# A hybrid SSD and gated-conv block on one core: gates beside the scans, sums of y in the merge, first loads by three queues, order at seams

## The chip, the core and the metric

The kernel runs on one core of a Trainium2 chip. The metric is the device time of one execution in microseconds (us). TensorE (PE) multiplies matrices, VectorE (DVE) and ScalarE (ACT) work element by element, GpSimd (POOL) and SyncE (SP) mainly issue transfers here; ACT can issue transfers too. Each engine runs its own instructions strictly in the order in which they were written. Where one needs another's result it waits on a semaphore, and everything behind it on its engine waits with it.

## What is computed

One block over 1024 tokens of width 1024, all in float32 (from the reference, cut):

```
u = rmsnorm(h) @ w_in
z, xbc, dt, s_b, s_c, s_x, g_a, g_b = split(u)
xbc = silu(conv(xbc)); y = scan(xbc, dt) + d_skip * xs
y = y * silu(z)
yg = y.reshape(4 groups); y = yg * rsqrt(mean(yg * yg) + eps) * w
branch_a = y @ w_ssd_proj
branch_b = (s_b * conv(s_c * s_x)) @ w_sconv_proj
h = h + (sigmoid(g_a) * branch_a + sigmoid(g_b) * branch_b) @ w_o
h = h + (silu(n @ w_gate) * (n @ w_up)) @ w_down       # n = rmsnorm(h)
return rmsnorm(h)
```

## The kernel before

**Matmuls.** A float32 product is three fp32r matmuls: each operand is split into an upper part (ACT, a copy) and a lower part (DVE, a subtraction; `split`, L73/L74 and L76/L77), and upper x upper, upper x lower and lower x upper are added (`mm3`, L81 to L83; `mmc`, L679 to L681). A matmul is 128x128 by 128x512.

**Pairs.** Most of the first projection is computed in `Pair`s: two slabs of 128 columns by Strassen's scheme with seven products in place of eight. A product is 4 blocks of 128 x 3 matmuls, so a pair takes 7 x 12 = 84 matmuls where two direct slabs take 96. The operands made of rows (B11, T1, T2 and so on) are split once by `put` and read by all pairs. The three first pairs (z 0 to 5) run with their products interleaved while the second half of the rows is still being turned and split (`second_half`, called from the loop over the first 21 products); the others follow one by one.

**Direct slabs and the scan.** 20 slabs are computed directly (`direct_tile`): z 12 to 15 and the 16 slabs of the two gates. Beside them runs the scan: 4 groups x 8 chunks of 128 tokens are 32 items of two parts each (`part1`, `part2`), a generator from which `direct_tile` takes a step after a matmul triple whenever `due` has grown: `due = turn * 65 // (len(direct) * 16 - 4)`. After each half of a group (4 chunks) a `norm` generator starts: it loads z, multiplies, squares, sums over the group by PE (`pq`), makes 1/sqrt (`rstd_of`), turns it by PE (`prt`), writes it to memory and reads it back spread over all partitions (`rbc`), scales y with it (L543) and writes y (`y_g`). With the second half of a group it makes four sums of y for the Strassen scheme of the merge (L557) and writes them (`yt_d`, L558).

**The merge.** `ms` is a stream of chunks of 24 matmuls: 14 of `gv` (conv branch), 28 of `gy` (scan branch), then `go` (w_o). `ms.step()` loads four chunks ahead, splits two ahead (two operands, so two ACT copies and two DVE subtractions for each chunk) and does one chunk of matmuls. Between chunks `pump_scan` takes the last steps of the scan's generator, which by then only steps the norms: a fixed number of steps for each chunk. The products T1 to T4 of `gy` read the sums of y.

**FFN.** `first_half` and `second_half` of `ffn_phase` normalise the new rows (`h1_rows`: rows whose index is in `act` are scaled by ACT at L135, the others by DVE at L137), turn them (`fill`) and split them with `put`; the sums for T3 are made by DVE at L1205. At the end `finish` adds two halves of a row's sum of squares and takes the root; `fin` scales and stores the last four row blocks.

**The start.** x comes in eight tiles, four of them ahead of the rest; their squares are summed alternately on ACT and DVE (`rows_sq`, "avav"). SP issues, in order, four x tiles, the first pair's weights, four x tiles, two more weights, the weights for the time steps (`wdts`), three more weights. POOL issues the small vectors (tile `c`), which PE turns into columns (L1532, L1533).

**Storage.** Nearly all tiles of 512 KB come from one pool of 47 pages, so a tile that lives longer takes a page from others.

Of the kernel before, what the change touches and what calls it, by code (L numbers as in the profile page):

```python
# [8 lines left out]
F32 = mybir.dt.float32  # L9
# [30 lines left out]
def hybrid_block(ctx: ExitStack, tc: tile.TileContext, x, nmw, w_in, cw, cb, dtb, alog, dsk, snw,  # L40
# [116 lines left out]
    class Slab:  # L157
# [3 lines left out]

        def load(self):
            if self.st is None:
                self.st = page(self.s + "s", self.shape)
                nc.sync.dma_start(self.st, self.src)

# [60 lines left out]
    wdt_s = sp.tile([P, KT * H], F32, tag="eb", bufs=3, name="wdts").rearrange("p (k h) -> p k h", h=H)  # L227
    warm = cp.tile([P, 1], F32, name="warm")
    nc.scalar.activation(warm, epst, AF.Sqrt)
    for i in range(4):  # L230
        nc.sync.dma_start(xt[i], x[i * P:(i + 1) * P, :])

# [9 lines left out]

    def more_loads():
        for i in range(4, NT):
            nc.sync.dma_start(xt[i], x[i * P:(i + 1) * P, :])
    d2 = cp.tile([16, 2], F32, name="d2")
# [255 lines left out]
    def norm(g, hf, y0, y1):  # L502
# [38 lines left out]
        for r in range(4):  # L541
            z = ys[r // 2][:, r % 2]
            V.scalar_tensor_tensor(z, z, snc(4 * g + r), rbc, op0=ALU.mult, op1=ALU.mult)  # L543
# [12 lines left out]
        for t, a, b, f in ((t1, b11, b12, "T1"), (t2, t1, b22, "T2"), (b12, b12, b22, "T3"), (b21, b21, t2, "T4")):  # L556
            V.tensor_add(t, a, b)  # L557
# [401 lines left out]

    z_held = []  # L960

    def z_raw(i):
        def f(ps, hf):
            if hf == 0:
                z_held.append((i, page("gt")))
            nc.scalar.activation(z_held[-1][1][:, hf * 512:hf * 512 + 512], ps, AF.Copy)
            if hf and len(z_held) == 2:
                for k, t in z_held:
                    nc.scalar.activation(t, t, AF.Silu)
                    nc.scalar.dma_start(z_d[k], t)  # L970
                z_held.clear()
        return f

    direct = [(wslab(w_in, i * P), z_raw(i)) for i in range(12, 16)]
    for j in range(KT):
# [187 lines left out]
    def ffn_phase():  # L1163
# [19 lines left out]
        def first_half():  # L1183
            rows0 = h1_rows(0, (2, 3))
            yield
            yield
            yield from fill(rows0, raw0, 0, wcol)
            yield from put("B11", raw0[0])
            yield from put("B21", raw0[1])

        def second_half(rows):
            yield from fill(rows, raw1, 1, wcol)
            t1 = [page("t1", HB) for _ in range(2)]
            for k in range(2):
                V.tensor_add(t1[k], raw1[0][k], raw0[0][k])
            t2 = [page("t2", HB) for _ in range(2)]
            for k in range(2):
                V.scalar_tensor_tensor(t2[k], raw1[1][k], -1.0, t1[k], op0=ALU.mult, op1=ALU.subtract)
            raw0[0].clear()
            every(put("T2", t2))  # L1200
            yield
            every(put("T1", t1))
            yield
            for k in range(2):
                V.tensor_add(raw1[0][k], raw1[1][k], raw1[0][k])  # L1205
# [200 lines left out]

        def rstd2_of(ssq, n, s):

            shp = list(ssq.shape)
            r = sp.tile(shp, F32, tag="rr", name=nm(s + "r"))  # L1410
            nc.scalar.activation(r, ssq, AF.Sqrt, scale=1.0 / n, bias=epst)
            v = sp.tile(shp, F32, tag="rv", name=nm(s + "v"))
            V.tensor_scalar(v, ssq, 1.0 / n, EPS, op0=ALU.mult, op1=ALU.add)
            V.reciprocal(r, r)
            q = sp.tile(shp, F32, tag="rq", name=nm(s + "q"))
            V.tensor_mul(q, r, r)
# [4 lines left out]
        def finish(ms):  # L1421
            s = sp.tile([P, len(ms), 1], F32, tag="fss", name=nm("fss"))
            V.tensor_add(s, sq[:, ms[0]:ms[-1] + 1, 0:1], sq[:, ms[0]:ms[-1] + 1, 1:2])
            return rstd2_of(s.rearrange("p a b -> p (a b)"), D, "f")

# [55 lines left out]
        ds.ahead(len(ds.chunks), len(ds.chunks))  # L1481

        def fin(m):
            t = 4 + m
            r = finish(range(t, t + 1))
            nc.scalar.activation(fo[t][:, 512:1024], h1[t][:, 512:1024], AF.Copy, scale=r)
            out_rows(t, r, 0)
            nc.sync.dma_start(out[t * P:(t + 1) * P, :], fo[t])

# [6 lines left out]

    first[0].y.load()
    more_loads()
    for p in first[1:]:
        p.y.load()  # L1500
    nc.sync.dma_start(wdt_s, w_in[:, DT0:DT0 + H].rearrange("(k p) f -> p k f", p=P))
    for p in first:
        p.x.load()
    small_loads()
    loaded[0] = NF
# [21 lines left out]

    a0 = rows_sq(xt[0:4], "x", "avav")
    a1 = rows_acc(xt[4:8], "x")
    del xt  # L1530
    pc = bank("pc")
    nc.tensor.transpose(pc[:, 0:96], ra, ident[:96, :96])  # L1532
# [168 lines left out]
    ffn_phase()  # L1701


# [25 lines left out]
```

## Time and profile before

| | us |
|---|---|
| runs shown (3) | 1908.9, 1909.17, 1910.7 |
| median | 1909.17 |
| the profiled execution's own time | 1910.68 |
| its span (first to last instruction) | 1908.9 |
| PE busy | 1879.7 |
| DVE busy | 1299.4 |
| ACT busy | 970.6 |
| POOL busy | 169.7 |

The stages follow each other by PE's work: the start to about 80 us, pairs to 619, direct slabs with the scan to 952, the merge and w_o to about 1267, the FFN's first products to 1691, its last to 1901, and the final rows. A row of a timeline gives start, duration, engine, line and operation, out<-in and shape; in brackets the idle time before it and what ended that. A PE row's end is modelled: neighbouring matmuls overlap in the records, so their starts count.

### The profile page before, as it was taken

How to read it: one execution, taken by the hardware profiler on the slowest of the kernel's cores; microseconds unless marked ns; L12 is line 12 of the kernel's file. 1: busy time of each engine (PE TensorE's matmuls, PEld its weight loads, DVE VectorE, ACT ScalarE, POOL GpSimd, SP SyncE). 2: the span in 40 equal slices, each digit the busy share in tenths (PEclk: the TensorE clock that was granted, in tenths of full speed). 3: DMA queues.
4: the chain of work that ended last, by engine and by line, in shares of the span. 5: the costliest groups of instructions: out<-in, count | busy, mean ns of one | idle time of the engine just before them, and what ended most of it. 6: DMA issues, size and time to landing. Idle time of an engine off the chain costs nothing.

```text
span 1908.9 us, 24143 instructions
## 1 busy us (share of the span) xinstructions
PE 1879.7 (98%) x8905; PEld 1545.3 (81%) x8905; DVE 1299.4 (68%) x1688; ACT 970.6 (51%) x1541; POOL 169.7 (9%) x196
## 2 busy tenths in 40 slices
PE   7999999999999999999999999999999999999998
PEld 5688888888888888888878888887888888888886
DVE  7667878777785678889878548877444444456465
ACT  5545454444444987877665454464333333345333
POOL 1010111101100000101010000101211121100000
PEclk9999999999999999999999999999999999999999
DMA  5197999978959656778798665917988888867552
GB/s 181 48 275 173 240 230 236 240 187 226 264 149 288 223 194 219 251 250 269 261 321 311 226 208 203 229 80 171 215 193 220 195 193 192 232 257 286 190 196 110
DMA packets 341190, 411.97 MB, mean 216 GB/s; under 512 B 17384, under 2 KB 223936, under 8 KB 341072
## 3 DMA queue, kind: packets, MB, share of 16 engines
q1 hardware_dynamic: 284400, 308.59, 50.0%
q0 software_dynamic: 48608, 72.47, 20.9%
q10 hardware_dynamic: 8064, 29.36, 3.8%
q8 instruction: 70, 1.15, 0.2%
q14 instruction: 48, 0.39, 0.1%
HBM read 320.56 MB, written 143.15 MB: 243 GB/s over the span
## 4 chain that ended last, share of the span: by engine, by line
PE 92%; DVE 4%; ACT 2%; DMA 1%; issue 1%; SPq 0%; ACTq 0%; DVEq 0%
PE pb L679 5%; PE pb L680 5%; PE pb L681 5%; PE gb L679 5%; PE gb L680 5%; PE gb L681 5%; PE fb L681 4%; PE fb L679 4%; PE fb L680 4%; PE pr L81 4%; PE pr L83 4%; PE pr L82 4%; PE gd L679 4%; PE pd L679 4%; PE gd L681 4%; PE gd L680 4%
## 5 line engine op out<-in xcount | busy, mean ns | idle before, releaser
L77 DVE TENSOR_TENSOR wl<-ws,wh 128x1024 fp32r<-128x1024 f32 x77 | 94.0, 1221 | 121.6 <-ACT wh L76 121.6
L679 PE MATMUL gb<-qh,gh 128*128 128x512 f32 x432 | 169.1, 391 | 1.1 <-DVE h L1132 1.1
L680 PE MATMUL gb<-ql,gh 128*128 128x512 f32 x432 | 168.9, 391 | 0.0
L681 PE MATMUL gb<-qh,gl 128*128 128x512 f32 x432 | 168.7, 391 | 0.0
L681 PE MATMUL fb<-th,wl 128*128 128x512 f32 x352 | 137.1, 389 | 0.8 <-DVE wl L77 0.8
L679 PE MATMUL fb<-th,wh 128*128 128x512 f32 x352 | 137.1, 390 | 0.6 <-ACT wh L76 0.6
L680 PE MATMUL fb<-tl,wh 128*128 128x512 f32 x352 | 137.0, 389 | 0.0
L81 PE MATMUL pr<-th,wh 128*128 128x512 f32 x320 | 131.1, 410 | 0.0
L679 PE MATMUL gd<-qh,gh 128*128 128x512 f32 x324 | 126.0, 389 | 0.0
L680 PE MATMUL gd<-ql,gh 128*128 128x512 f32 x324 | 126.0, 389 | 0.0
L681 PE MATMUL gd<-qh,gl 128*128 128x512 f32 x324 | 126.0, 389 | 0.0
L83 PE MATMUL pr<-th,wl 128*128 128x512 f32 x320 | 125.1, 391 | 0.0
L82 PE MATMUL pr<-tl,wh 128*128 128x512 f32 x320 | 124.9, 390 | 0.0
L76 ACT ACTIVATE qh<-cb 128x1024 fp32r<-128x1024 f32 x98 | 99.8, 1018 | 38.0 <-PE gb L680 17.1
L77 DVE TENSOR_TENSOR ql<-cb,qh 128x1024 fp32r<-128x1024 f32 x98 | 115.6, 1180 | 1.6 <-ACT qh L76 1.4
L74 DVE SCALAR_TENSOR_TENSOR gl<-ca,gh 128x1024 fp32r<-128x1024 f32 (+1 forms) x60 | 70.5, 1174 | 49.0 <-ACT gh L73 49.0
L681 PE MATMUL fd<-th,wl 128*128 128x512 f32 x264 | 102.7, 389 | 0.0
L679 PE MATMUL fd<-th,wh 128*128 128x512 f32 x264 | 102.7, 389 | 0.0
L680 PE MATMUL fd<-tl,wh 128*128 128x512 f32 x264 | 102.7, 389 | 0.0
L679 PEld LDWEIGHTS gb<-qh,gh 128*128 128x128 f32 x432 | 81.5, 189 | 18.4 <-DVE h L1132 1.4
L679 PE MATMUL pb<-th,wh 128*128 128x512 f32 x240 | 94.4, 394 | 1.0 <-ACT u L894 1.0
L681 PEld LDWEIGHTS gb<-qh,gl 128*128 128x128 f32 x432 | 81.5, 189 | 17.1
(324 smaller groups left out, 4702.3 us busy)
## 6 DMA issues: line engine op xcount, KB each, us to landing
ws<-in_w_in_dram SPq DMA_DIRECT2D x80, 512.0 KB, 6.3
ws<-in_w_gate_dram SPq DMA_DIRECT2D x77, 256.0 KB, 3.9
ws<-in_w_up_dram SPq DMA_DIRECT2D x77, 256.0 KB, 4.4
ca<-u_d SPq DMA_DIRECT2D x35, 512.0 KB, 5.3
ab<-ac_d SPq DMA_DIRECT2D x32, 512.0 KB, 6.0
xbc_g<-cv ACTq DMA_DIRECT2D x24, 512.0 KB, 7.0
ws<-ws POOLq DMA_DIRECT2D x22, 512.0 KB, 6.4
wd_d<-in_w_down_dram SPq DMA_DIRECT2D x20, 512.0 KB, 10.8
```

Of the source, the lines that this page charges most:

```text
L74: nc.vector.scalar_tensor_tensor(lo, src, -1.0, hi.bitcast(F32), op0=ALU.mult, op1=ALU.subtract)
L76: nc.scalar.activation(hi, src, AF.Copy)
L77: nc.vector.tensor_sub(lo, src, hi.bitcast(F32))
L81: nc.tensor.matmul(o, lh, rh, start=first, stop=False)
L82: nc.tensor.matmul(o, lh, rl, start=False, stop=False)
L83: nc.tensor.matmul(o, ll, rh, start=False, stop=last)
L679: nc.tensor.matmul(o, lh, rh, start=first, stop=False, skip_group_check=True)
L680: nc.tensor.matmul(o, lh, rl, start=False, stop=False, skip_group_check=True)
L681: nc.tensor.matmul(o, ll, rh, start=False, stop=last, skip_group_check=True)
```

## The change

- Two more `Pair`s compute z 12 to 15; `direct` holds only the 16 gate slabs. The scan's 65 steps are spread over 252 turns instead of 316.
- The four sums of y move out of `norm` into `y_sums`. Only the last group's are still made there. For the other three groups both halves of y are written to memory, their pages go free, and `late_sums` reads them back during the merge (four tiles of 512 KB for a group, POOL's queue), makes the sums and writes them. It takes one step in each of chunks 10 to 13 and two in each later one; the next group's read-back is issued with the second of a group's four sums.
- `step_norms` steps the newer norm first.
- First loads: x tiles 1 and 3 go out on ACT's queue, tiles 4 to 7 too, between ACT's squares; the second and third weights, `wdts` and three further weights go out on POOL's queue.
- `put("T2")` at the start is done with step 7 of the turning and not one step later.
- `h1_rows(0, (3,))`: ACT scales one row block and DVE three; before, two each.
- The FFN's T3 is summed by a transfer on POOL's queue that adds to its destination.
- The last rows: `fin` gives the other half's sum of squares to the root as its bias (`known`), so that the addition of `finish` is not needed; the last row block is stored in two halves by SP and ACT.

```diff
-                if hf == 0 or r > 1:
+                if hf == 0 or r > 1 or g < G - 1:
...
+        if g < G - 1:
+            return
         if hf == 0:
             kept[g] = ys
             return
-
-        b11, b21 = kept.pop(g)
-        b12, b22 = ys
+        yield from y_sums(g, kept.pop(g), ys)
+
+    def y_sums(g, y_0, y_1):
+
+        b11, b21 = y_0
+        b12, b22 = y_1
         t1, t2 = page("s1", HB), page("s2", HB)
         for t, a, b, f in ((t1, b11, b12, "T1"), (t2, t1, b22, "T2"), (b12, b12, b22, "T3"), (b21, b21, t2, "T4")):
             V.tensor_add(t, a, b)
             nc.gpsimd.dma_start(yt_d[f][256 * g:256 * g + 256, :].rearrange("(k p) f -> p k f", p=P), t)
             yield
 
+    def late_sums():
+        def back(g):
+            r = []
+            for hf in range(2):
+                r.append([page("yb", HB) for _ in range(2)])
+                for i in range(2):
+                    nc.gpsimd.dma_start(r[hf][i], y_g[g][256 * i:256 * i + 256, hf * 512:hf * 512 + 512]
+                                        .rearrange("(r p) l -> p r l", p=P))
+            return r
+        nxt = back(0)
+        yield
+        for g in range(G - 1):
+            now, nxt = nxt, None
+            for i, _ in enumerate(y_sums(g, *now)):
+                if i == 1 and g + 1 < G - 1:
+                    nxt = back(g + 1)
+                yield
+            del now
...
-            for n in list(norms):
+            for n in norms[::-1]:
...
-    z_pairs = [Pair(i * P, (silu_z(i), silu_z(i + 1))) for i in range(0, 12, 2)]
+    z_pairs = [Pair(i * P, (silu_z(i), silu_z(i + 1))) for i in range(0, 16, 2)]
...
-    direct = [(wslab(w_in, i * P), z_raw(i)) for i in range(12, 16)]
+    direct = []
...
-            rows0 = h1_rows(0, (2, 3))
+            rows0 = h1_rows(0, (3,))
...
+            for k in range(2):
+                nc.gpsimd.dma_start(raw1[0][k], raw1[1][k], accum_op=ALU.add)
             every(put("T2", t2))
             yield
             every(put("T1", t1))
             yield
-            for k in range(2):
-                V.tensor_add(raw1[0][k], raw1[1][k], raw1[0][k])
             every(put("T3", raw1[0]))
...
+            r = rstd2_of(sq[:, t, 0:1], known[:, m:m + 1])
...
+            if k == 7:
+                every(put("T2", t2))
+            yield
-        every(put("T2", t2))
...
+    late = late_sums()
     while ms.at < len(gv.chunks) + len(gy.chunks):
...
         ms.step()
+        for _ in range(0 if ms.at < 10 else 1 if ms.at < 14 else 2):
+            next(late, None)
         pump_scan({1: 2, 2: 2, 4: 3}.get(ms.at, 1 if ms.at < 12 else 2))
         pump(2)
         pump_aux()
+    every(late)
```

First place: PE at the start of the merge, where the last norm's sum over the group (`pq`) and the turning of its root (`prt`) stand among the chunks' matmuls (`gd`, `gb`). Before, with 24 rows of `gb` between the first and the last of these, of which the ends are shown:

```order
L681 MATMUL gd_8318<-qh_8245,gl_8242 128x512
L527 MATMUL pq_8378<-ones,sa_8281 128x1 x4
L679 MATMUL gb_8196<-qh_8295,gh_8291 128x512
L680 MATMUL gb_8196<-ql_8296,gh_8291 128x512
...
L681 MATMUL gb_8217<-qh_8295,gl_8292 128x512
L532 MATMUL prt_8432<-ident,gr_8385 4x128
L679 MATMUL gb_8196<-qh_8339,gh_8335 128x512
```

And with the change:

```order
L708 MATMUL gd_8299<-qh_8232,gl_8229 128x512
L528 MATMUL pq_8356<-ones,sa_8220 128x1 x4
L533 MATMUL prt_8375<-ident,gr_8363 4x128
L706 MATMUL gb_8185<-qh_8276,gh_8272 128x512
L707 MATMUL gb_8185<-ql_8277,gh_8272 128x512
```

The chunk of 24 matmuls that stood between `pq` and `prt` now stands behind both.

Second place: DVE in the merge, at the chunks that read the first sums of y. `gl` and `ql` are the lower parts of a chunk's two operands, `yb` the tiles that are read back, `s1` and `s2` the first two sums of a group. Before:

```order
L77 TENSOR_TENSOR gl_8909<-ca_8828,gh_8908 128x1024
L77 TENSOR_TENSOR ql_8913<-cb_8830,qh_8912 128x1024
L77 TENSOR_TENSOR gl_8945<-ca_8868,gh_8944 128x1024
L77 TENSOR_TENSOR ql_8949<-cb_8870,qh_8948 128x1024
L77 TENSOR_TENSOR gl_8987<-ca_8904,gh_8986 128x1024
L77 TENSOR_TENSOR ql_8991<-cb_8906,qh_8990 128x1024
```

With the change (the tiles' numbers are those of two counters):

```order
L563 TENSOR_TENSOR yb_1369_8736<-yb_1369_8736,s2_1387_8836 128x1024
L563 TENSOR_TENSOR s1_1408_8929<-yb_1398_8881,yb_1400_8885 128x1024
L77 TENSOR_TENSOR gl_1413_8938<-ca_1388_8839,gh_1412_8937 128x1024
L77 TENSOR_TENSOR ql_1415_8942<-cb_1389_8841,qh_1414_8941 128x1024
L563 TENSOR_TENSOR s2_1409_8930<-s1_1408_8929,yb_1401_8886 128x1024
L563 TENSOR_TENSOR yb_1400_8885<-yb_1400_8885,yb_1401_8886 128x1024
L77 TENSOR_TENSOR gl_1419_8978<-ca_1402_8891,gh_1418_8977 128x1024
L77 TENSOR_TENSOR ql_1421_8982<-cb_1403_8893,qh_1420_8981 128x1024
```

The last sum of the second group and the first of the third stand directly ahead of one chunk's splits, two further sums ahead of the next chunk's.

Third place: ACT at the start. `xn` are the squares of x's tiles, `cols` the columns of the small vectors. Before:

```order
L229 ACT_TABLE_LOAD
L229 ACTIVATE warm<-epst 128x1
L117 ACTIVATE xn_206,xss_205<-x_85 128x1024
L117 ACTIVATE xn_210,xss_205<-x_87 128x1024
L1534 ACTIVATE cols<-pc_215 128x176
```

With the change:

```order
L230 DMA x_86<-in_x_dram 128x1024
L230 DMA x_88<-in_x_dram 128x1024
L231 ACT_TABLE_LOAD
L231 ACTIVATE warm<-epst 128x1
L117 ACTIVATE xn_185,xss_184<-x_85 128x1024
L245 DMA x_89<-in_x_dram 128x1024
L245 DMA x_90<-in_x_dram 128x1024
L117 ACTIVATE xn_191,xss_184<-x_87 128x1024
L245 DMA x_91<-in_x_dram 128x1024
L245 DMA x_92<-in_x_dram 128x1024
L1560 ACTIVATE cols<-pc_215 128x176
```

Six issues of x tiles stand among ACT's first instructions, two ahead of its table load.

More of the change, by code (lines that the diff above doesn't have):

```diff
@@ L228, in hybrid_block @@
     warm = cp.tile([P, 1], F32, name="warm")
+    for i in range(4):
+        (nc.scalar if i % 2 else nc.sync).dma_start(xt[i], x[i * P:(i + 1) * P, :])
     nc.scalar.activation(warm, epst, AF.Sqrt)
-    for i in range(4):
-        nc.sync.dma_start(xt[i], x[i * P:(i + 1) * P, :])
     consts = page("c")
@@ L241, in hybrid_block, with more_loads @@
     nc.gpsimd.dma_start(rb[56:80, :], scw[0].rearrange("k (i p) -> (k i) p", p=P))
-    def more_loads():
-        for i in range(4, NT):
-            nc.sync.dma_start(xt[i], x[i * P:(i + 1) * P, :])
+    def more_loads(i):
+        for i in (i, i + 1):
+            nc.scalar.dma_start(xt[i], x[i * P:(i + 1) * P, :])
     d2 = cp.tile([16, 2], F32, name="d2")
@@ L1423, in finish @@
             V.tensor_add(s, sq[:, ms[0]:ms[-1] + 1, 0:1], sq[:, ms[0]:ms[-1] + 1, 1:2])
-            return rstd2_of(s.rearrange("p a b -> p (a b)"), D, "f")
+            return rstd2_of(s.rearrange("p a b -> p (a b)"), epst)
         def out_rows(t, r, n):
@@ L1481, in ffn_phase @@
         ds.ahead(len(ds.chunks), len(ds.chunks))
+        known = sp.tile([P, 4], F32, tag="rv", name=nm("fk"))
+        V.tensor_scalar(known.unsqueeze(2), sq[:, 4:8, 1:2], 1.0 / D, EPS, op0=ALU.mult, op1=ALU.add)
         def fin(m):
             t = 4 + m
-            r = finish(range(t, t + 1))
+            r = rstd2_of(sq[:, t, 0:1], known[:, m:m + 1])
             nc.scalar.activation(fo[t][:, 512:1024], h1[t][:, 512:1024], AF.Copy, scale=r)
             out_rows(t, r, 0)
-            nc.sync.dma_start(out[t * P:(t + 1) * P, :], fo[t])
+            if m < 3:
+                nc.sync.dma_start(out[t * P:(t + 1) * P, :], fo[t])
+            else:
+                nc.scalar.dma_start(out[t * P:(t + 1) * P, 512:1024], fo[t][:, 512:1024])
+                nc.sync.dma_start(out[t * P:(t + 1) * P, 0:512], fo[t][:, 0:512])
         for m in range(4):
@@ L1497, in hybrid_block @@
     first[0].y.load()
[L1498 to L1504, printed above, removed]
     loaded[0] = NF
@@ L1526, in steps_pe @@
                 j == len(todo) - 1 and part == 1)
-    a0 = rows_sq(xt[0:4], "x", "avav")
+    a0 = rows_acc(xt[0:4], "x")
+    rows_sq_on("a", a0, "x")
+    more_loads(4)
+    rows_sq_on("v", a0, "x")
+    rows_sq_on("a", a0, "x")
+    more_loads(6)
+    first[1].y.load(nc.gpsimd)
+    nc.gpsimd.dma_start(wdt_s, w_in[:, DT0:DT0 + H].rearrange("(k p) f -> p k f", p=P))
+    first[2].y.load(nc.gpsimd)
+    rows_sq_on("v", a0, "x")
     a1 = rows_acc(xt[4:8], "x")
     del xt
+    for p in first:
+        p.x.load(nc.gpsimd)
+    small_loads()
     pc = bank("pc")
```

28 lines of the change are left out of this document (8 added, 20 removed).

## The prediction, made before the changed kernel was run

> **What bounds the kernel now.** I read the busy shares first, then the chain that ended last, then TensorE's rows one by one, its waits, and last the other engines stage by stage.
>
> ```profile
> span 1908.9 us, 24143 instructions
> PE 1879.7 (98%) x8905; PEld 1545.3 (81%) x8905; DVE 1299.4 (68%) x1688; ACT 970.6 (51%) x1541; POOL 169.7 (9%) x196
> PE 92%; DVE 4%; ACT 2%; DMA 1%; issue 1%; SPq 0%; ACTq 0%; DVEq 0%
> 706.15 0.39 PE L82 MATMUL pr<-tl,wh 128*128 128x512 f32 x1
> 706.38 0.39 PE L83 MATMUL pr<-th,wl 128*128 128x512 f32 x1
> PE pc L1532 <- DMA c<-in_ssd_conv_w_dram: 8.0, 1, 8.0
> PE prt L532 <- DVE gr L107: 2.1, 1, 2.1
> 984.20:987.60 3.40, 3.40 (x9) 2.64 (x9) 3.40 (x4) 2.39 (x4) 0.53 (x1) 0.50 0.93 260
> ```
>
> TensorE (PE) is the bound: 92% of the chain is its own work. A matmul's row says 0.39 us, but the starts are 0.23 us apart, 0.227 over longer stretches, so a matmul costs 0.227. What can be won is the number of matmuls, and the few waits: 8.0 us before the first work, 2.1 us for `prt` in the merge, and smaller ones below. The last row shows what the `prt` wait drew after it: a window of 3.4 us in which the granted clock (the last number but two) was 0.50. At half speed it costs 3.4 x 0.5 = 1.7 us, so this place costs close to 4 us.
>
> **1. Four z slabs go to pairs.**
>
> ```profile
> L81 PE MATMUL pr<-th,wh 128*128 128x512 f32 x320 | 131.1, 410 | 0.0
> ```
>
> Direct slabs have 320 x 3 = 960 matmuls for 20 slabs, 48 each. A pair makes two slabs with 7 products of 4 blocks of 3, 84. Four slabs go from 192 to 168. 24 x 0.227 = **-5.44 us**. The two pairs' sums, splits and loads lie among 20 pairs that run without stalls; the order of PE's rows (8076 before, 8052 now) gives the same 24.
>
> **2. The scan has 768 matmuls to hide under instead of 960.**
>
> ```profile
> 619.00:952.00 333.00, 333.00 (x2061) 274.97 (x2060) 277.90 (x472) 263.82 (x611) 19.72 (x30) 1.00 0.73 238
> L557 DVE TENSOR_TENSOR s<-y,y 128x1024 f32<-128x1024 f32 x3 | 3.6, 1216 | 0.0
> L990 DVE TENSOR_TENSOR wl<-ws,wh 128x1024 fp32r<-128x1024 f32 x19 | 23.1, 1218 | 0.5 <-ACT wh L987 0.5
> 628.77 0.68 DVE L450 TENSOR_TENSOR xw<-xx,xw 128x512 fp32r<-128x512 f32 x1
> 630.79 0.39 PE L81 MATMUL pst<-xw,bh 128*128 128x512 f32 x1
> ```
>
> The columns after the window are its length, then busy us of PE, weight loads, DVE, ACT, POOL. The 333 us shrink by 192 x 0.227 = 43.6 to 289. DVE had 278 us; the nine sums of y that lie here leave it (L557, 1.216 each, in four groups of which the first is shown: 10.9), and four of the 19 splits at L990 (4 x 1.22 = 4.9). 262 of 289 is 91%. ACT had 264; without the z copies, their silu and four splits (three passes over 128x1024 for each slab, estimated at the 1.04 us of the row at 13.90 below: 12.5) some 251, 87%. So the scan fits, without room: single items will run above 100% for 10 to 20 us, paid from the lead that DVE's tiles of the later items have. The first item has little: the row at 628.77 ends at 629.45, and the matmuls that read `xw` begin at 630.79. They now stand three steps of 0.68 us earlier. I take **+0.4 us**, between 0 and +3, the upper end if each of four starts of a group is late like that (4 x 0.7).
>
> **3. Twelve sums of y come into the merge, with twelve read-backs.**
>
> ```profile
> 1011.00:1046.00 35.00, 35.00 (x156) 28.96 (x156) 34.30 (x36) 17.88 (x19) 3.59 (x5) 1.00 0.91 326
> 1023.00:1046.00 23.00, 23.00 (x104) 19.02 (x103) 23.00 (x24) 8.96 (x9) 2.14 (x3) 1.00 1.01 370
> 1057.49 1.23 DVE L77 TENSOR_TENSOR gl<-ca,gh 128x1024 fp32r<-128x1024 f32 x1 [11.05 <-ACT gh L76]
> DMA to landing us min/median/max: 4.1/7.5/9.9
> DMA to landing us min/median/max: 3.1/5.8/8.7
> ```
>
> Twelve sums of 1.22 us are 14.6 us of DVE. In the chunks into which they are put DVE is busy 34.3 of 35 us, because it runs ahead of PE there; the 11.05 us idle before 1057.49 is that lead. The sums eat it, and the splits of the next chunks (two of 1.2 us per chunk of 24 x 0.227 = 5.45 us) become just ready. The sum itself is then hidden; what isn't is a wait inside it. In the order of DVE the first sum of the third group stands ahead of two splits, and its read-back is issued on POOL's queue only behind a write of the second group's second sum, about one chunk earlier. The last two rows are the landing times of the nearest transfers, of 512 KB too: writes of the sums (L558) and of y (L547). I take 6 to 8 us from issue to landing against the 5.45 us of a chunk; DVE then stands 0.6 to 2.5 us, with the 1 us or so of margin before and a second read-back behind, PE 0.9 to 3.6. Bounds: 0, if DVE keeps 4 us of its lead, and +5, a wait of 9.9 - 5.45 = 4.45 us and a piece of halved clock. I take **+1.8 us**. Nothing below 0, since no wait of PE is there now to be removed.
>
> **4. The `prt` wait at the start of the merge.**
>
> ```profile
> 974.49 1.05 PE L527 MATMUL pq<-ones,sa 128*128 128x1 f32 x8
> 983.22 0.27 PE L532 MATMUL prt<-ident,gr 128*4 128x128 f32 x1 [2.12 <-DVE gr L107]
> 979.12 2.74 DVE L543 SCALAR_TENSOR_TENSOR y<-y,cols,rbc 128x512 f32<-128x512 f32 x4 [2.89 <-DMA rbc<-rs_d]
> 981.77 0.15 DVE L99 TENSOR_SCALAR gv<-pq 128x4 f32<-128x4 f32 x1
> 983.01 0.16 DVE L107 TENSOR_TENSOR gr<-gr,gq 128x4 f32<-128x4 f32 x1
> ```
>
> Before, `prt` stood 24 matmuls (5.4 us) behind `pq`, and still waited: DVE, in order, had stood 2.89 us for `rbc` and then did four L543 before the rstd. In the new order `prt` stands right behind `pq`, so PE waits the whole rstd, 983.17 - 981.77 = 1.4 us plus the handovers at both ends, 1.6 to 2.2. That is no less than 2.1. But the two norms are stepped newer first, so that of the older norm's four L543 two stand three splits' time ahead of the rstd and two behind it; and POOL has no sums' writes ahead of the older norm's little transfer, so `rbc` should be there. Whether the half clock follows again is open (0 to 1.7). 2.0 + 0.9 against 2.1 + 1.7: **-1.0 us**, between -2.4 (a short wait, full clock) and +3 (`rbc` late again with DVE standing for 2.9 more, and the clock). The Trainium skill ("TensorE: Matmul & The Clock Gate", the table of "Why this matters for your kernels") asks for no idle gaps above some 3 us; by it a wait of 2 us would cost no clock. The trace disagrees, as 2.12 us idle was followed by 3.4 us at 0.50. By the page the term would be -1.8.
>
> **5. First loads on three queues.**
>
> ```profile
> PE pc L1533 <- DMA c<-in_sconv_w_dram: 1.9, 1, 1.9
> 5.00:6.00 1.00, 0.00 (x0) 0.00 (x0) 0.50 (x1) 0.25 (x2) 1.00 (x3) 1.00 0.59 178
> 7.00:8.00 1.00, 0.00 (x0) 0.01 (x1) 0.00 (x0) 0.00 (x0) 0.00 (x0) 1.00 1.03 399
> 8.41 1.06 ACT L117 ACTIVATE xn<-x 128x1024 f32<-128x1024 f32 x1 [3.16 <-DMA x<-in_x_dram]
> 13.90 1.04 ACT L864 ACTIVATE wh<-ws 128x1024 fp32r<-128x1024 f32 x1
> 19.93 0.42 ACT L1512 ACTIVATE wdt<-wdts 128x256 fp32r<-128x256 f32 x1 [0.68 <-DMA wdts<-in_w_in_dram]
> ```
>
> ACT's second x tile (the third of four) let it start at 8.41, after 3.16 us of waiting; PE's first transposes wait for constants, 8.0 us and then 1.9 more. At 5 to 6 us the transfers stand at 0.59 of their share, then at 1.03. Filling that hole brings the last x tile at most 0.4 to 0.8 us earlier. Against it: the weights of `ws`, read at 13.90, now stand third on SP and share with later x tiles; if they come 1.5 us later, PE's first products do. I take **0**, from -1.7 (hole filled, and the 0.68 us wait for the time-step weights gone too) to +2. The Trainium skill ("DMA: Bandwidth & Descriptors", "Rules for kernel authors") says that spreading over SP, ACT and GpSimd gives no bandwidth, only issue time; the 0.59 is either late issue, which spreading mends, or not, and no run here yet tells which. By the page the gain is at most the issue time.
>
> **6 and 7. Two seams.**
>
> ```profile
> PE pb L680 <- DVE tl L77: 1.6, 3, 0.8
> PE pb L679 <- ACT th L76: 0.5, 1, 0.5
> PE gb L679 <- DVE h L1132: 1.1, 1, 1.1
> 1248.41 2.19 ACT L135 ACTIVATE hn<-h,nr 128x1024 f32<-128x1024 f32 x2 [1.10 <-DVE nr L107]
> 1250.51 1.04 ACT L73 ACTIVATE gh<-mc 128x1024 fp32r<-128x1024 f32 x1
> 1251.58 1.23 DVE L74 SCALAR_TENSOR_TENSOR gl<-mc,gh 128x1024 fp32r<-128x1024 f32 x1 [1.81 <-ACT gh L73]
> 1253.86 2.47 DVE L1132 TENSOR_TENSOR h<-h,gb 128x512 f32<-128x512 f32 x4
> ```
>
> T2's split one step earlier: PE waits 0.5 for its upper part and about 1.0 of the 1.6 for its lower part. With 12 or more matmuls of lead most goes: **-1.0**, from -1.65 to 0 (ACT and DVE are as late either way). At 1253 PE waits 1.1 us for L1132, behind two splits, the first of which stood 1.81 us for ACT; ACT had done two rows of 1.1 us at L135. One goes to DVE, which was idle in those 1.81 us: ACT is 1.1 earlier, DVE too: **-1.05**, from -1.3 to 0.
>
> **8. The rest.**
>
> ```profile
> 1295.53 2.35 DVE L1205 TENSOR_TENSOR br<-br,br 128x1024 f32<-128x1024 f32 x2
> 1903.25 0.16 DVE L1423 TENSOR_TENSOR fss<-sqf 128x1 f32<-128x1 f32 x1 [0.79 <-ACT fo L1405]
> 1903.44 0.29 ACT L1411 ACTIVATE fr<-fss,epst 128x1 f32<-128x1 f32 x1 [0.23 <-DVE fss L1423]
> ```
>
> T3's two sums (2.35 us of DVE) become an accumulating transfer: DVE idles behind them, and T3 is used many slots later: 0, at worst +1 if its landing is late. At the end the sum of two squares and the wait on DVE for it go (L1423's 0.16 us and a handover of 0.23), and the last row leaves by two queues: **-0.3**, from -0.6 to +0.2.
>
> Sum: -5.44 + 0.4 + 1.8 - 1.0 + 0 - 1.0 - 1.05 - 0.3 = **-6.6 us**. The profiled execution took 1910.68 (span 1908.9 and 1.8 around it); the sum made on it gives 1904.1. The median of the runs shown is 1909.17, 1.5 below, the profile's own at their upper end; the median becomes 1902.6.
>
> **The rivals.**
> - **The merge gives it back.** The third group's wait is 3.6 us and draws 1.7 of half clock, and `prt` does no better than before (no -1.0): 1902.6 + 3.5 + 1.0 = 1907.1. For it: the transfers stand at 1.01 of their share from 1023 to 1046, before 12 read-backs and three writes of 512 KB come in. Against: DVE's lead of 11 us. Within 0.2%.
> - **Slower: the first sum of every group waits.** Each of the three holds the splits behind it until its read-back lands, 3 us each, with half a clock window of 1.7 behind two of them: 9 + 3.4 instead of 1.8, so 1902.6 + 10.6 = 1913.2. It decides from a landing of 8.5 us on (5.45 and 3). The writes' 9.9 speaks for it, the median of 5.8 and the first two groups' earlier prefetch against.
> - **It doesn't do what it says:** DVE at 91% and ACT at 87% are too much for an order written ahead, and PE waits in each of the eight later items for 0.4 us: 1902.6 + 3.2 = 1905.8, hardly a gain. The mean shares speak against, the first item's 0.7 for.
> - **The head gains in full**, and all seams: -1.7, -0.9 more: 1900.0, with no wait in the merge 1898.2.
>
> **How the numbers follow.** Forecast 0.50 (1900.5 to 1905), head and merge in full 0.19, merge gives back 0.14, scan not hidden 0.09, slower 0.08. Some 0.2%, 3.8 us, is what a measurement of this kernel can tell from no change: faster means below 1905.4, slower above 1913. Faster: 0.50 + 0.19 and a part of the scan case, 0.74; same 0.20; slower 0.06. The range goes from 1897.5 to 1908.5: it leaves out the slower case and the ends of the two others.
>
> **What would show it.** 8052 rows of PE; between 619 and the merge no wait of PE longer than 1 us; one short wait for `prt` right behind `pq`; the read-back's wait, if any, at DVE's L563 with two splits behind it; the waits at 57 and 1253 gone. It is wrong if the windows of the scan show idle PE above 3 us in sum, if POOL's read-backs land later than 8.5 us after issue, or if PE's first product starts later than now.

## The result and the profile after

The changed kernel takes **1923.72 us** (median of 6 runs, 1922.7 to 1924.87) against 1909.24 us (6 runs): a ratio of 1.0076, 95% interval 1.0066 to 1.0086. It is 14.5 us slower, where 6.6 us faster was forecast. The profiled execution took 1923.23 us.

The page of the changed kernel: span, busy time, and the share of each engine in the chain that ended last.

```profile
span 1921.2 us, 24162 instructions
PE 1879.1 (98%) x8881; PEld 1543.4 (80%) x8881; DVE 1309.7 (68%) x1704; ACT 966.9 (50%) x1542; POOL 188.7 (10%) x219
PE 83%; DVE 7%; ACT 5%; issue 3%; DMA 3%; POOL 0%; ACTq 0%; SPq 0%; DVEq 0%; POOLq 0%
```

PE has the 24 matmuls less (8881 records for 8905), but its share of the chain fell from 92% to 83%. Some rows of the waits of PE in the changed kernel (engine, tile and line waiting, who ended it: us in sum, times, longest):

```profile
PE pc L1558 <- DMA c<-in_ssd_conv_w_dram: 8.2, 1, 8.2
PE gd L707 <- DVE ql L77: 7.9, 1, 7.9
PE poff L476 <- DVE st L485: 5.4, 1, 5.4
PE prt L533 <- DVE gr L107: 2.0, 1, 2.0
PE pb L707 <- DVE tl L77: 1.4, 2, 0.8
```

Two long ones are new: 7.9 us in the merge and 5.4 us at the end of the scan. Four short ones beside the scan, 2.2 us in sum, are new too. To see what each stage lost, take the start of its first matmul from PE's timeline. For the changed kernel: the first product, the first direct slab, the chunks 1, 15 and 21 of the merge, and the FFN.

```profile
18.18 0.48 PE L706 MATMUL pb<-th,wh 128*128 128x512 f32 x1
654.67 0.39 PE L81 MATMUL pr<-th,wh 128*128 128x512 f32 x1
955.14 0.39 PE L706 MATMUL gb<-qh,gh 128*128 128x512 f32 x1
1035.91 0.39 PE L706 MATMUL gb<-qh,gh 128*128 128x512 f32 x1
1079.81 0.39 PE L706 MATMUL gd<-qh,gh 128*128 128x512 f32 x1
1279.56 0.39 PE L706 MATMUL fb<-th,wh 128*128 128x512 f32 x1
```

The differences of such starts, for before, the change and every experiment (all times in us; "pairs" and "direct" hold other numbers of matmuls before: 168 are 38.1 us more in the pairs now, 192 are 43.6 us less in the direct slabs):

| kernel | to first product | pairs | direct, scan | chunks 1-14 | chunks 15-20 | w_o, norm | span |
|---|---|---|---|---|---|---|---|
| before | 19.33 | 599.64 | 333.59 | 81.39 | 32.64 | 81.11 | 1908.9 |
| changed | 18.18 | 636.49 | 300.47 | 80.77 | 43.90 | 80.07 | 1921.2 |
| e1_split | 18.26 | 636.53 | 293.51 | 82.81 | 44.13 | 80.09 | 1916.6 |
| e2_third_later | 17.51 | 636.91 | 301.57 | 80.48 | 37.75 | 80.10 | 1915.6 |
| e3_sums_back | 18.58 | 636.06 | 304.46 | 80.51 | 32.64 | 80.07 | 1913.7 |
| e4_prt | 19.43 | 637.78 | 301.06 | 77.37 | 41.91 | 80.07 | 1919.0 |
| e5_all | 18.28 | 636.73 | 293.57 | 78.52 | 33.61 | 80.11 | 1902.2 |
| e6_nolate | 17.96 | 636.87 | 298.52 | 78.82 | 32.64 | 80.11 | 1906.3 |
| e7_seams_back | 18.33 | 638.98 | 300.63 | 82.79 | 42.73 | 81.15 | 1925.9 |
| e8_copies | 18.55 | 636.41 | 300.55 | 81.03 | 32.64 | 80.09 | 1911.6 |
| e9_t2 | 18.45 | 637.31 | 293.53 | 78.72 | 33.62 | 80.10 | 1903.1 |
| e10_loads | 19.52 | 636.00 | 293.55 | 78.56 | 33.61 | 80.05 | 1902.2 |
| e12_z | 18.79 | 598.09 | 333.58 | 77.37 | 33.65 | 80.07 | 1902.9 |

Chunks 21 to 42 of the merge take 119.7 us in each (120.6 in e8_copies), the FFN up to the last matmul 633.8 to 633.9, the rest 7.4 to 7.8. Of the changed kernel's 12.3 us of span, the direct stage has 10.5 (333.59 - 43.6 would be 290.0) and chunks 15 to 20 have 11.3; everything else together, the 24 matmuls (5.4 us) included, gained 9.5.

**At the end of the scan**, DVE's timeline in the changed kernel, from the last work for item 30 on:

```profile
933.54 0.76 DVE L497 TENSOR_TENSOR y<-y,xx 128x256 f32<-128x256 f32 x2
937.53 1.22 DVE L74 SCALAR_TENSOR_TENSOR gl<-ca,gh 128x1024 fp32r<-128x1024 f32 x1 [3.22 <-ACT gh L73]
938.67 1.22 DVE L77 TENSOR_TENSOR ql<-cb,qh 128x1024 fp32r<-128x1024 f32 x1
939.80 0.68 DVE L442 TENSOR_TENSOR xx<-pxt,dtt 128x512 f32<-128x512 f32 x1
...
944.93 0.68 DVE L485 TENSOR_TENSOR st<-st,pst 128x512 f32<-128x512 f32 x1
```

DVE stands 3.22 us for the upper part of the merge's first chunk (`gh`), which ACT makes behind the eviction of a gate slab (L683). PE wasn't late there: that slab's last matmul had started at 930.27. ACT was: from 928.42 to 936.04 it was busy for 7.58 of 7.62 us, with the scan's own work and this eviction.

```profile
935.46 0.58 ACT L683 ACTIVATE gt<-pr 128x512 f32<-128x512 f32 x1
936.44 1.06 ACT L73 ACTIVATE gh<-ca 128x1024 fp32r<-128x1024 f32 x1 [0.40 <-ACT gt L683]
```

The split takes DVE 2.3 us more, and only then come the last item's part 1 (L442) and the state (L485) for which PE waits at the last item's `poff`:

```profile
945.75 0.55 PE L476 MATMUL poff<-bc,st 128*128 128x128 f32 x1 [5.42 <-DVE st L485]
```

Before, the last item's part 1 (there L441) stood ahead of this split, and ACT had time to wait for PE:

```profile
934.30 0.69 DVE L441 TENSOR_TENSOR xx<-pxt,dtt 128x512 f32<-128x512 f32 x1 [2.58 <-PE pxt L426]
938.29 1.22 DVE L74 SCALAR_TENSOR_TENSOR gl<-ca,gh 128x1024 fp32r<-128x1024 f32 x1
939.42 1.22 DVE L77 TENSOR_TENSOR ql<-cb,qh 128x1024 fp32r<-128x1024 f32 x1
941.76 0.67 DVE L484 TENSOR_TENSOR st<-st,pst 128x512 f32<-128x512 f32 x1
935.91 0.60 ACT L656 ACTIVATE gt<-pr 128x512 f32<-128x512 f32 x1 [2.54 <-PE pr L83]
```

Counted in PE's matmul triples of the direct slabs, the last item's part 1 stood behind number 302 before, two ahead of the last slab's start (304). Now it stands behind 241, one behind that start (240), and the split is tied to the start.

**In the merge**, DVE's timeline in the changed kernel; a split (L77) makes two operands' lower parts, L563 is a late sum:

```profile
1050.85 1.22 DVE L77 TENSOR_TENSOR ql<-cb,qh 128x1024 fp32r<-128x1024 f32 x1
1051.98 1.22 DVE L563 TENSOR_TENSOR yb<-yb,s 128x1024 f32<-128x1024 f32 x1
1063.10 1.23 DVE L563 TENSOR_TENSOR s<-yb,yb 128x1024 f32<-128x1024 f32 x1 [9.90 <-issue]
1064.25 1.22 DVE L77 TENSOR_TENSOR gl<-ca,gh 128x1024 fp32r<-128x1024 f32 x1
1065.38 1.22 DVE L77 TENSOR_TENSOR ql<-cb,qh 128x1024 fp32r<-128x1024 f32 x1
```

The third group's first sum stands 9.90 us, and the two splits behind it are what PE waits for. The row of the sum names no engine or transfer that ended its wait, but the landings do. The sum reads the first and the third of its group's four read-backs. POOL issued the four from 1049.66 on, 0.7 us apart, and they landed 9.5, 10.7, 11.9 and 13.2 us after their own issues:

```profile
DMA to landing us min/median/max: 9.5/11.3/13.2
```

DVE came to the sum at 1053.20, 3.5 us behind the first issue. The third tile landed at 1063.02, 13.4 us behind it, and the sum began at 1063.10. The landing times of all twelve read-backs, and the stretch 1036 to 1085 of the changed kernel (busy PE, weight loads, DVE, ACT, POOL, then the granted clock, the transfers' share and GB/s):

```profile
DMA to landing us min/median/max: 4.0/10.5/13.8
1036.00:1085.00 49.00, 40.74 (x168) 32.86 (x167) 34.06 (x32) 21.27 (x23) 9.97 (x14) 0.90 1.04 413
```

And the same stretch before:

```profile
1036.00:1085.00 49.00, 49.00 (x218) 40.58 (x217) 29.03 (x29) 21.80 (x24) 0.00 (x0) 1.00 0.72 245
```

The transfers' share was 0.72 before and is 1.04 now: twelve times 512 KB read back and more of y written. Landing, 5.8 and 7.5 us in the median for the rows I had gone by, is 10.5 here. The share alone doesn't explain that: before, the four writes of the last group's sums landed within 7.0 to 9.3 us in a stretch at 1.01.

```profile
DMA to landing us min/median/max: 7.0/8.0/9.3
1020.00:1041.00 21.00, 21.00 (x95) 17.38 (x94) 21.00 (x24) 10.17 (x10) 2.87 (x4) 1.00 1.01 369
```

Those were issued 1.1 to 5.8 us apart, the read-backs 0.7 us apart, and of the read-backs each landed later than the one ahead of it. No run issues them singly, so how much of the landing is the burst's and how much the load's isn't shown.

Around and behind each of the long waits the clock is halved (the last number but two):

```profile
945.25:949.00 3.75, 3.25 (x22) 3.05 (x24) 3.64 (x7) 0.00 (x0) 0.38 (x1) 0.54 0.08 9
979.50:983.00 3.50, 3.06 (x8) 2.48 (x9) 3.45 (x6) 2.65 (x4) 1.25 (x2) 0.52 0.70 260
1061.50:1071.75 10.25, 5.09 (x12) 4.03 (x13) 8.65 (x8) 2.11 (x2) 2.15 (x3) 0.50 1.04 412
```

### The profile page after: what moved, and what is told of

Its sections match the earlier page's. It is cut to its first block, busy times and chain, and to the rows that moved or that the text cites. A ratio compares the mean times of both kernels' runs of the same rounds, so it can differ in the third digit from the quotient of the medians.

```text
span 1921.2 us, 24162 instructions
## 1 busy us (share of the span) xinstructions
PE 1879.1 (98%) x8881; PEld 1543.4 (80%) x8881; DVE 1309.7 (68%) x1704; ACT 966.9 (50%) x1542; POOL 188.7 (10%) x219
## 3 DMA queue, kind: packets, MB, share of 16 engines
q8 instruction: 70, 1.15, 0.2%
## 4 chain that ended last, share of the span: by engine, by line
PE 83%; DVE 7%; ACT 5%; issue 3%; DMA 3%; POOL 0%; ACTq 0%; SPq 0%; DVEq 0%; POOLq 0%
PE pb L706 6%; PE pb L707 6%; PE pb L708 6%; PE gb L706 4%; PE gb L707 4%; PE gb L708 4%; PE pd L706 4%; PE pd L707 4%; PE pd L708 4%; PE fb L708 4%; PE fb L707 4%; PE fb L706 4%; PE gd L707 3%; PE gd L708 3%; PE gd L706 3%; PE fd L707 3%
## 5 line engine op out<-in xcount | busy, mean ns | idle before, releaser
L77 DVE TENSOR_TENSOR wl<-ws,wh 128x1024 fp32r<-128x1024 f32 x77 | 94.0, 1221 | 121.6 <-ACT wh L76 121.6
L77 DVE TENSOR_TENSOR ql<-cb,qh 128x1024 fp32r<-128x1024 f32 x98 | 115.7, 1181 | 1.7 <-ACT qh L76 1.7
L81 PE MATMUL pr<-th,wh 128*128 128x512 f32 x256 | 106.2, 415 | 0.0
L891 ACT ACTIVATE wh<-ws 128x1024 fp32r<-128x1024 f32 x64 | 67.8, 1059 | 67.2 <-DVE ws L878 62.9
L707 PE MATMUL pb<-tl,wh 128*128 128x512 f32 x256 | 99.9, 390 | 1.4 <-DVE tl L77 1.4
L706 PE MATMUL pb<-th,wh 128*128 128x512 f32 x256 | 100.6, 393 | 0.5 <-ACT u L921 0.5
L83 PE MATMUL pr<-th,wl 128*128 128x512 f32 x256 | 100.3, 392 | 0.7 <-DVE wl L1003 0.7
L708 PE MATMUL pb<-th,wk 128*128 128x512 f32 x256 | 99.7, 390 | 0.3 <-DVE wk L895 0.3
```

The source lines that it names most:

```text
L77: nc.vector.tensor_sub(lo, src, hi.bitcast(F32))
L81: nc.tensor.matmul(o, lh, rh, start=first, stop=False)
L83: nc.tensor.matmul(o, ll, rh, start=False, stop=last)
L706: nc.tensor.matmul(o, lh, rh, start=first, stop=False, skip_group_check=True)
L707: nc.tensor.matmul(o, lh, rl, start=False, stop=False, skip_group_check=True)
L708: nc.tensor.matmul(o, ll, rh, start=False, stop=last, skip_group_check=True)
```

## The experiments

Each starts from the changed kernel unless another is named.

**e1_split.** The first chunk's split goes into the last direct slab, behind the last item's part 1 and the state for which PE waited.

```diff
-        ms.ahead(i - len(direct) + 4, i - len(direct) + 2)
+        ms.ahead(i - len(direct) + 4, 0)
...
+                if i + 1 == len(direct) and (hf, k) == (0, 5):
+                    ms.ahead(0, 1)
```

> The changed kernel, but the split of the merge's first chunk stands in the last direct slab behind the last item's first part and the part after it, not at the start of that slab. Theory A (the place): PE's 5.4 us wait for the scan's state at 940 comes from DVE standing 3.2 us for that split's upper part while the last items are queued behind it; it goes, with the half clock behind it, and the direct stage falls from 300.5 us to 292 to 294. Theory B (no room: DVE at 90% of a shorter stage): the wait stays at 3 us or more and the stage at 297 or more. Nothing else moves; total 6 to 8 us below the changed kernel by A, under 3 by B.

1918.48 us; ratio to before 1.0044 (1.0022 to 1.0067). The direct stage is 293.51, 7.0 us shorter: the 5.4 us and 1.6 of the half clock, as theory A has it. DVE's timeline there, without the wait:

```profile
933.69 0.76 DVE L497 TENSOR_TENSOR y<-y,xx 128x256 f32<-128x256 f32 x2
934.37 0.68 DVE L442 TENSOR_TENSOR xx<-pxt,dtt 128x512 f32<-128x512 f32 x1
...
939.54 0.68 DVE L485 TENSOR_TENSOR st<-st,pst 128x512 f32<-128x512 f32 x1
```

The state is ready 5.4 us earlier, before PE asks for it. ACT is as busy in these microseconds as in the changed kernel, so the place alone ends the wait. Chunks 1 to 14 lose 2.0 us of the gain: PE comes earlier to `pq` and waits 0.8 us there, and the wait at `prt` stays (2.1 us). In all the kernel is 5.2 us faster than the changed one, under the 6 to 8 expected.

**e2_third_later.** One step of the late sums less behind chunk 16.

```diff
-        for _ in range(0 if ms.at < 10 else 1 if ms.at < 14 else 2):
+        for _ in range(0 if ms.at < 10 else 1 if ms.at < 14 or ms.at == 16 else 2):
```

> The changed kernel, but the first two sums of the third group are made one chunk later, behind the splits of the chunk that waited 8.0 us; no transfer is taken away. Theory A (the place in DVE's order): the splits no longer wait for the read-back, chunks 15 to 20 of the merge fall from 43.9 us to 33 to 35 (32.6 before the change), total 9 to 11 us below the changed kernel. Theory B (the transfers' share is at 1.0, so the chunks' own loads are late too): PE's wait only changes its name, 40 us or more.

1921.12 us over three runs (1917.38 to 1921.37, the profiled one the lowest); 1.0055 (1.0032 to 1.0078). Chunks 15 to 20 take 37.75 us, neither 33 to 35 nor 40, and the total is 2.6 us lower, not 9 to 11: a part of the wait only moved on by one chunk. The landing was still 7.7 to 11.6 us from the issue, the sum waited 5.8 us, the splits of the next chunk stood behind it, and PE waited 2.8 us there. It shows that the place counts, but not that the place is enough.

**e3_sums_back.** All sums beside the scan, as before (`norm` as before, no `late_sums`).

> The changed kernel with all four groups' sums of y made beside the scan as before, with no read-back. By both theories of the merge chunks 15 to 20 return to 32.6 us. For the scan: nine more sums, 10.9 us of DVE in the direct stage, 272 of 300. Theory A (the place of the split): the direct stage gets no or little longer, 300 to 303. Theory B (no room on DVE): it grows by most of the 10.9, to 306 to 312. Total 1910 to 1914 by A, 1916 to 1924 by B.

1915.89 us; 1.0036 (1.002 to 1.0052). The merge is back at 32.64: the 11.3 us are the late sums'. The direct stage is 304.46, between the two theories, as is the total. PE's two long waits there:

```profile
PE poff L476 <- ACT st L483: 3.7, 2, 3.3
PE poff L476 <- DVE st L485: 3.0, 1, 3.0
```

The second is the one of e1_split again, a little shorter. The first is a lack of room, as the timelines of DVE and ACT have it: DVE works without a pause from 882 to 896, one of the sums stands ahead of the next item's first product (L438), ACT waits 1.60 us for that product, and the state's copy (L483) stands behind it on ACT.

**e4_prt.** `{1: 2, 2: 2, 4: 3}` becomes `{1: 2, 2: 2, 4: 2}`: `prt` stands 24 matmuls behind `pq` again.

> The changed kernel with two steps of the norms in place of three behind the fourth chunk of the merge, so that the last norm's transpose stands one chunk of 24 matmuls behind its sum again. If its 2.0 us wait and the half clock of 4 us behind it come from standing directly behind the sum, both go: chunks 1 to 14 fall from 80.8 us to 77 to 78. If the root is late for another reason (the spread-out copy, DVE's order), they stay at 80 or more. The norms' last steps are one chunk later, so that a new wait for the sums of the fourth group may show in chunks 20 to 30.

1919.33 us; 1.0053 (1.003 to 1.0076). Chunks 1 to 14 fall to 77.37, 3.4 us less, wait and half clock gone. In the changed kernel, then in this one:

```profile
977.03 0.95 PE L528 MATMUL pq<-ones,sa 128*128 128x1 f32 x8
979.94 0.37 PE L533 MATMUL prt<-ident,gr 128*4 128x128 f32 x1 [1.96 <-DVE gr L107]
```

```profile
980.16 0.95 PE L528 MATMUL pq<-ones,sa 128*128 128x1 f32 x8
986.55 0.27 PE L533 MATMUL prt<-ident,gr 128*4 128x128 f32 x1
```

No wait is left in the second. The newer norm first, with the older distance, is what helps; the shorter distance took most of it back. e6_nolate below, with this order and distance but the sums beside the scan as before, has no wait at `prt` either.

**e8_copies.** The sums go, the transfers stay: what is read back is written out as it is.

```diff
-            for i, _ in enumerate(y_sums(g, *now)):
+            for i, t in enumerate((now[0][0], now[0][1], now[1][0], now[1][1])):
+                nc.gpsimd.dma_start(yt_d[f"T{i + 1}"][256 * g:256 * g + 256, :].rearrange("(k p) f -> p k f", p=P), t)
```

> The changed kernel with its twelve late sums left out of the computation: the tiles read back are themselves written to where the sums went, so that the transfers stay, in number and size, and DVE has nothing to wait for. Theory A (the place: splits queued behind a sum that waits): no wait in the merge, chunks 15 to 20 at 32.6 to 33.5 us. Theory B (the transfers at a share of 1.0 delay the chunks' own operands too): 36 us or more, with the waits named after ca or cb.

1913.73 us; 1.0024 (1.0012 to 1.0035). Chunks 15 to 20 take 32.64, with no wait. The landing times of the read-backs, and the same stretch as above:

```profile
DMA to landing us min/median/max: 4.6/12.9/15.1
1036.00:1085.00 49.00, 49.00 (x218) 40.41 (x217) 24.12 (x26) 22.76 (x25) 7.85 (x11) 1.00 1.04 412
```

The transfers are as dense (1.04) and land still later (12.9), yet PE doesn't wait: the chunks' own operands are loaded four ahead. So dense transfers and late landings alone don't cost; the cost is the in-order wait on DVE. The run also lacks the sums' 14.6 us of DVE and their two pages, so it doesn't tell waiting from working on DVE; e5_all, which has both, does.

**e5_all.** e1_split and e4_prt, and the late sums begun behind chunk 7, one a chunk.

```diff
-        for _ in range(0 if ms.at < 10 else 1 if ms.at < 14 else 2):
+        for _ in range(0 if ms.at < 7 else 1):
```

> The changed kernel with the first chunk's split later (as in the first run), two norm steps behind the fourth chunk (as in the fourth), and the late sums begun three chunks earlier, behind chunk 7, one sum a chunk throughout. Theory A (place and lead: a read-back then has two chunks and more from issue to use, and the transfers' share is 0.4 to 1.0 there): the direct stage 293 to 294, chunks 1 to 14 77 to 79, chunks 15 to 20 33 to 35; in all 19 to 21 us below the changed kernel, 1902 to 1906. Theory B (the added transfers fill the queues wherever they stand, and pages are short): chunks 1 to 20 together stay at 118 or more (124.7 in the changed kernel, 114.0 before), total above 1908.

**1903.94 us** (6 runs, 1903.58 to 1904.7); ratio to before **0.9972** (0.9958 to 0.9985). It beats both kernels, the one before by 4.8 us. Chunks 15 to 20 take 33.61 with the same transfers, as its landing times and the stretch 1005 to 1085 show:

```profile
DMA to landing us min/median/max: 7.4/9.8/11.8
1005.00:1085.00 80.00, 79.32 (x351) 65.34 (x350) 67.87 (x68) 37.59 (x40) 13.58 (x19) 1.00 1.04 411
```

A landing of 9.8 us does little harm where two sums of the group before, one a chunk, lie between issue and use: for the third group that is 12.0 us, and DVE still stands 0.42 us for the third tile, so there is no margin. The first group's four landed in 7.4 to 11.6 us at a share of 0.88, the third's in 7.7 to 11.8 at 1.04: landing went with the place in the burst more than with the share.

**e6_nolate.** e1_split, e4_prt, and the sums beside the scan as in e3_sums_back.

> The changed kernel with the sums of y made beside the scan as before (as in the third run), the first chunk's split later and two norm steps behind the fourth chunk. Theory A: of the third run's two waits in the direct stage the one at 946 (3.1 us and its half clock) goes, the one at 889 (3.5 us, for a copy of the state on ACT) stays; the direct stage falls from 304.5 to 299 to 301, chunks 1 to 14 to 77 to 79, chunks 15 to 20 stay at 32.6: total 1906 to 1909. Theory B (DVE has no room with the sums): the wait moves to another item, 303 or more.

1908.21 us; 0.9997 (0.9986 to 1.0008). The wait of 3.0 went, that of 3.3 for ACT's copy stayed, as theory A has it (298.52, just under its 299). Against e5_all, the direct stage has 4.95 us more and chunks 1 to 20 have 0.67 less: moving the sums is worth 4.3 us, if they are put where nothing waits behind them.

**e7_seams_back.** Head, T2, scaled rows, T3 and the tail as before, all at once.

> The changed kernel with everything outside the direct stage and the merge undone: first loads, T2's split, the scaled rows, the FFN's T3 and the last rows as before. Each term by itself, from the stages' lengths: PE's first product from 18.2 back to 19.3 us; the pairs behind it longer by 1.0 to 1.6 us by T2; w_o and the rows behind it from 80.1 back to 81.1; the tail 7.7 to 7.8 either way. In all 2.5 to 4 us above the changed kernel. If T2's wait is instead replaced by one for the first loads' order, the pairs don't change.

1926.62 us, 2.9 more than the changed kernel; 1.0084 (1.0054 to 1.0113). w_o and norm go back to 81.15 (the term of 1.05 is right), the pairs are 2.5 us longer, not 1.0 to 1.6. There are two runs only, and their profile also differs by 2.0 us in chunks 1 to 14, which the edit doesn't touch. The first product comes at 18.33, not at 19.3: one profile's start doesn't settle the first loads.

**e9_t2, e10_loads.** e5_all with only T2's split, or only the first loads, put back.

> The fifth run's kernel (all three places mended) with only T2's split put back to where it was before. PE's waits for T2's upper and lower part at about 56 us (0.6 and 1.0) come back: the first direct matmul 1.3 to 1.7 us later than in the fifth run's kernel (655.0), total 1905 to 1906. If the wait before was due to the rows and not to the order of the split, nothing moves.

1905.28 us, 1.3 above e5_all; 0.9981 (0.9971 to 0.9991). T2's waits at 56 are back; in the profiles the first direct matmul is only 0.75 us later (655.76 for 655.01), not 1.3 to 1.7.

> The fifth run's kernel with only the first loads as before: x on SP's queue alone, the weights behind it. If three queues bring the first tiles earlier, PE's first product comes 0.5 to 1.2 us later than with them (18.2 us in the changed kernel's profile, 19.3 before), and the first direct matmul as much. If issuing engines add no bandwidth and the constants' landing sets the start, the first product stays at 18.0 to 18.6 and nothing else moves by more than 0.3 us.

1904.16 us, 0.2 above e5_all and inside its runs' spread; 0.9974 (0.9963 to 0.9984). In the profiles the first product is 1.2 us later (19.52 for 18.28), but the first direct matmul only 0.5. That the loads make this difference isn't shown: with three queues the first product came anywhere from 17.51 to 19.43 us in ten kernels (e4_prt has the latest), with the older loads at 18.33, 19.33 and 19.52.

**e12_z.** e5_all with z 12 to 15 back among the direct slabs, and three norm steps behind the fourth chunk.

> The fifth run's kernel with z 12 to 15 back among the direct slabs (three norm steps behind the fourth chunk as before, since the scan then has one step left over): 24 matmuls more, 5.4 us, under a scan that has 43.6 us more to hide in. If the shorter stretch costs only its small waits (2.9 us in sum in the fifth run's kernel against none before), the total is 2 to 3.5 us above the fifth run's, 1905.5 to 1907.5. If the short stretch loses what the pairs win, it is within 1 us of it.

1905.37 us, 1.4 above e5_all, just below the range; 0.9985 (0.9975 to 0.9994). The direct stage is 333.58, as before, with no wait; with 43.6 us taken off e5_all's would be 290.0, and is 293.57. So of the 5.4 us that two more pairs save, the tighter scan takes back 3.6, mostly in e5_all's four waits in the scan:

```profile
PE poff L476 <- ACT st L483: 1.2, 2, 0.8
PE pr L83 <- DVE wl L1003: 0.7, 1, 0.7
PE pst L82 <- DVE xw L451: 0.4, 1, 0.4
```

With the handovers around them they make some 2.8 us by the starts of the matmuls; the rest isn't traced to a place. Chunks 1 to 14 also take 1.15 us less than in e5_all, so the 1.4 us isn't the price of the pairs alone.

## Why the prediction was wrong, point by point

1. **Two more pairs, -5.44:** right, 24 matmuls less.
2. **The scan's cover, +0.4, at most +3:** here the prediction failed first; it was +10.5. The step that failed is the one from mean shares to "the scan fits". The shares forecast, DVE 91% and ACT 87% of 289 us, were no lower than the measured ones (261.5 and 243.8 us busy in 300), and the first item's wait came as forecast (0.4). But the term had no wait in it for the order at the end of the scan. Spreading 65 steps over 252 turns instead of 316 moves them against everything that is tied to a slab, and the first chunk's split is tied to the last slab's start. The last item's part 1 now stood behind it on DVE, just where ACT had no pause for 7.6 us. The prediction named such stretches above 100% and paid them from DVE's lead; DVE couldn't use its lead, as it stood idle for ACT. e1_split puts a price on the place: 7.0 of the 10.5. The remaining 3.5 are, for the most part, the four short waits of PE, the term that was forecast at 0.4 and at most 3. That the split had come ahead of part 1 can be read from the order of DVE's rows, without any time.
3. **The late sums, +1.8, at most +5:** the mechanism was named, at its very place (the third group's first sum, two splits behind it), and mis-sized: +11.3. Two sizes were wrong. The lead from the first issue to DVE's coming to the sum was taken as a chunk of 5.45 us and was 3.5. The landing was taken as that of one transfer, 6 to 8 us; the sum needs the third of four issued together, and that landed 13.4 us behind the first issue. So DVE stood 9.9 us, not 0.6 to 2.5, and PE 7.9. Of the half clock around it 5.1 us fell on work, 2.6 us of loss, in place of "a piece". The slower rival, with a chance of 0.08, came near in price: 9 + 3.4 = 12.4 us for the merge against 11.3 measured. Its condition, landings above 8.5 us, held for ten of the twelve read-backs, but the price was to come from all three groups, and one was enough; that the sizes nearly agree is luck. Even the upper bounds of terms 2 and 3 together would only have given 1908.4.
4. **`prt`, -1.0:** -0.6, inside its bounds: the wait of 1.96 us came as worked out, and the half clock followed. e4_prt shows what was to be had there, -4.0 against before. In e2_third_later and e3_sums_back 1.50 us idle behind 0.95 us of one-column matmuls were followed by half clock. The Trainium skill ("TensorE: Matmul & The Clock Gate", the table of "Why this matters for your kernels") warns of idle gaps above some 3 us. The measurement decides against that bound here.
5. **First loads, 0:** right in the total (0.2 us by e10_loads, inside the spread). The Trainium skill ("DMA: Bandwidth & Descriptors", "Rules for kernel authors") has it that spreading over issuing engines only saves issue time. The total agrees with that rule.
6. **T2, -1.0:** right, -1.3 by e9_t2. **7. Scaled rows, -1.05:** right, 81.11 to 80.07.
8. **Tail, -0.3:** missed, if by little; the last issue comes 0.4 us earlier behind the last matmul (3.79 for 4.15), but the rest of the span after the last matmul is 7.82 for 7.69: nothing gained. T3 by a transfer: 0, as forecast (the FFN takes 633.83 us for 633.84).

Of the three signs of being wrong that the prediction names, two came: PE's idle time beside the scan was 7.6 us in sum (5.4 and 2.2), and ten of the twelve read-backs landed later than 8.5 us after issue.

## What to carry to other kernels

When work that is spread by a counter is squeezed, look at which instructions tied to something else (a slab's start, a chunk) it now falls behind, on each in-order engine; a mean share (91% of DVE, 87% of ACT) says nothing about that. When several read-backs are issued together, go by the landing of the last one that the first reader needs, not by that of a single transfer, and issue them so early that it is over before anything useful queues behind that reader. Issuing first the two tiles that the first sum needs is the obvious next try; no run here does it. Two late waits in a kernel bound by PE cost more than they last, since a slow stretch of the clock lay around or behind each (7.0 us for 5.4, 10.5 for 7.9).

## What the runs showed of the hardware

The slow stretches come in steps of 3.4 us: one step behind waits of 1.50, 1.96 and 2.12 us (two behind much the same wait in e7_seams_back), one or two around waits of 2.8 to 5.4, and two or three around those of 6.7 to 8.1 us, part of it while PE still waited. The waits of 1.13 us (before, at 1253) and 1.16 us (e6_nolate, at 959) had no such stretch. Transfers at a share of 1.04 for 49 and 80 us (e8_copies, e5_all; 411 and 412 GB/s) cost PE nothing and 0.7 us, with operands asked for four chunks ahead. Four read-backs of 512 KB issued 0.7 us apart landed one behind the other, 9.5, 10.7, 11.9 and 13.2 us after their own issues in the changed kernel's third group.
